# Feed-forward blocks of a four-layer hybrid network: gate and up products made token-first or feature-first

## The chip, the cores and the metric

The kernel runs on one core of one Trainium2 chip, as a single program without communication. The metric is the device time of one execution in microseconds; less is better. A core has a matrix engine (TensorE, PE in the profile, with its weight loads listed apart as PEld), a vector engine (VectorE, DVE), a scalar engine (ScalarE, ACT), GpSimd (POOL), and a queue that issues DMA transfers (SyncE, SP).

## The reference, cut to what matters

```python
D_MODEL = 1024; SEQ = 256; DEPTH = 4; D_FF = 2816; FFN_HALF = 0.5

def swiglu(x, w_gate, w_up, w_down):
    return (jax.nn.silu(x @ w_gate) * (x @ w_up)) @ w_down

def reference(x, norm_pre, norm_post, ffn_w_gate, ffn_w_up, ffn_w_down, ...):
    for i in range(DEPTH):
        f = swiglu(rms_norm(x, norm_pre[i, 0]), ffn_w_gate[i, 0], ffn_w_up[i, 0], ffn_w_down[i, 0])
        x = x + FFN_HALF * rms_norm(f, norm_post[i, 0])
        hn = rms_norm(x, norm_pre[i, 1])
        ...  # one of three attention mixers m, by i % 3
        x = x + rms_norm(m, norm_post[i, 1])
        f = swiglu(rms_norm(x, norm_pre[i, 2]), ffn_w_gate[i, 1], ffn_w_up[i, 1], ffn_w_down[i, 1])
        x = x + FFN_HALF * rms_norm(f, norm_post[i, 2])
    return x
```

There are 256 tokens, a model width of 1024 and 2816 inner features. Each layer has two feed-forward blocks, so the program has eight, with an attention mixer between the two blocks of a layer (dilated, differential, sliding-window, and dilated again).

## The kernel before, in words

**Precision.** Every float32 operand of a matmul is split into a high and a low part of type fp32r, and `mm3` (lines 173 to 176) makes one product from three matmuls: high by high (L174), high by low (L175), low by high (L176). The first operand of `mm3` is the stationary one and its second is the moving one. In the profile's names the moving operand stands first: `gu<-hi,xT` has weights moving and xT stationary, `qk<-xT,hi` has xT moving and weights stationary.

**Weights.** They come in units of 128 x 2048 values (1 MB) in an order fixed in advance. `load_next` puts a DMA on the SP queue into one of three `raw` buffers; `split_next` makes `hi` on ACT (L141) and `lo` on DVE, or on POOL for some units (L142), in two pieces (four on POOL), into four rotating buffers each. `done(i)` is called after the last matmul of a unit: it splits the unit four ahead into the buffers that come free, and loads the next.

**A feed-forward block.** `norm_tr` transposes the normed input to `xT` (high and low, 8 row groups of 128 model features by 256 tokens each). `new_xT` starts it 48 elements into its buffer in the mixers and at 0 in the feed-forward blocks. `ffn` then works through the inner features in six chunks c, five of 512 and a last one of 256. Within a chunk it makes the gate product for the two halves of the tokens, t = 0 and 1 (PSUM banks of tag mm, three of them), then the up product (banks of tag s, two). xT is stationary, 128 tokens at a time, and 512 columns of weights move: 8 row groups x 3 matmuls for each of two halves and two products, 96 matmuls per chunk. `gate` applies silu on ACT (L360), `up` multiplies on DVE (L365) to `h`, with tokens on the partitions. `transposes` turns `h` back on TensorE (four transposes of 128 columns for each half, two in the last chunk, L373), and ACT and DVE write the result as `hTh` and `hTl` (L376, L377). The transposes of chunk c - 1 are issued in chunk c between the first and the second weight unit of its gate product; those of the last chunk come after the first unit of `closing`.

**closing** multiplies hT (stationary) by the 11 units of the down weights (512 columns moving, `acc`), adds to the residual `x` and prepares the next stage's norm. It is the same for feed-forward blocks and mixers.

**Mixers.** They issue their input projections in pieces between attention work. Query and key projections (`qk`) have the weights stationary and 256 columns of xT moving; value projections (`v`) of the dilated mixer have xT stationary and 384 columns of weights moving. Score products (`sc`), transposes (`tp`) and value products (`o`) stand between these pieces. Each engine has its instructions in one order, fixed when the program is built.

Of the kernel before, what the change touches and what calls it, by code (L numbers as in the profile page):

```python
# [8 lines left out]
F32 = mybir.dt.float32  # L9
F32R = mybir.dt.float32r  # L10
BF16 = mybir.dt.bfloat16
AF = mybir.ActivationFunctionType
ALU = mybir.AluOpType

P = 128
SEQ = 256
D = 1024
DFF = 2816
KD = D // P
# [26 lines left out]
def tile_network(  # L46
# [27 lines left out]
    act, dve, pe, pool = nc.scalar, nc.vector, nc.tensor, nc.gpsimd  # L74
# [7 lines left out]
    def bank(tag, name):  # L82
        return ps.tile([P, 512], F32, tag=tag, name=name, bufs={"mm": 3, "s": 2, "tr": 2, "o": 1}[tag])
# [61 lines left out]
    def take(n=1):  # L145
        i = state["use"]
        state["use"] += n
        return list(range(i, i + n))
# [3 lines left out]
    def pump(n=99):  # L152
        while pending and n:
            n -= 1
            i = pending.pop(0)
            split_next()
            load_next()
            for f in hooks.pop(i, []):
                f()

    def done(i, later=False):
        his.pop(i)
        los.pop(i)
        pending.append(i)
        if not later:
            pump()

    def wview(i, k):
        w = units[i].shape[-1]
        return (his[i][:, :w].rearrange("p (k n) -> p k n", k=k),  # L170
                los[i][:, :w].rearrange("p (k n) -> p k n", k=k))

    def mm3(o, a, b, first, last):
        pe.matmul(o, lhsT=a[0], rhs=b[0], start=first, stop=False)  # L174
        pe.matmul(o, lhsT=a[0], rhs=b[1], start=False, stop=False)  # L175
        pe.matmul(o, lhsT=a[1], rhs=b[0], start=False, stop=last)  # L176
# [18 lines left out]
    xT = {}  # L195

    NX, NH = KD * SEQ, KF * SEQ

    def two(z, o, n):

        return [z[:, o + i * n:o + (i + 1) * n].rearrange("p (k n) -> p k n", n=SEQ) for i in range(2)]

    def new_xT(s):
        z = actp.tile([P, 2 * NX + 64], F32R, tag="xT", name="xT")
        xT["h"], xT["l"] = two(z, 48 if s % 3 == 1 else 0, NX)

    def xt(k, t):
        sl = slice(t * P, (t + 1) * P) if t is not None else slice(0, SEQ)
# [15 lines left out]
    hn_of = {}  # L224

    def norm_elem(t, s, parts=1):

        ss = small.tile([P, 1], F32, tag="ssx", name="ssx")
        hn = actp.tile([P, D], F32, tag="w", name="hn", bufs=3)
        act.activation(out=hn, in_=x[:, t], func=AF.Square, scale=1.0 / 32.0, accum_out=ss)  # L230
        r = rstd_of(ss, None)
        state["norm"] = state["rstd"]
        for c in range(parts):
            cs = slice(c * D // parts, (c + 1) * D // parts)
            i = dve.scalar_tensor_tensor(out=hn[:, cs], in0=x[:, t, cs], scalar=r, in1=gains["pre", s][:, cs],
                                     op0=ALU.mult, op1=ALU.mult)
        hn_of[t] = hn, s
        return i

    def boundary_elem(t, s, acc, mid):  # L240
# [30 lines left out]
            return norm_tr_(t)  # L271

    def norm_tr_(t):
        hn, s = hn_of.pop(t)
        if t == 0:
            new_xT(s)
        for g in range(2):
            tp = bank("tr", "tp")
            for j in range(4):
                k = 4 * g + j  # L280
                pe.transpose(tp[:, j * P:(j + 1) * P], hn[:, k * P:(k + 1) * P], ident)
            tv = tp.rearrange("p (i n) -> p i n", i=4)
            h = xT["h"][:, 4 * g:4 * g + 4, t * P:(t + 1) * P]
            i = act.copy(out=h, in_=tv)
            dve.tensor_tensor(out=xT["l"][:, 4 * g:4 * g + 4, t * P:(t + 1) * P], in0=tv,
                              in1=h.bitcast(F32), op=ALU.subtract)
        return i
# [56 lines left out]
    def ffn(layer, which):  # L344
        s = 3 * layer + 2 * which
        with ExitStack() as c:
            fp = c.enter_context(tc.tile_pool(name="ffn", bufs=2, reuse_waits="tile"))
            hTh, hTl = two(fp.tile([P, 2 * NH], F32R, name="hT", bufs=1), 0, NH)
            hs = {}

            def mm_unit(i, k, k0, o, t, mid=None):
                wh, wl = wview(i, k)
                for kk in range(k):
                    if mid and kk == k // 2:
                        mid()
                    mm3(o, xt(k0 + kk, t), (wh[:, kk], wl[:, kk]), k0 + kk == 0, k0 + kk == KD - 1)

            def gate(c, t, g, w):
                sg = fp.tile([P, 512], F32, tag="sg", name="sg")
                act.activation(out=sg[:, :w], in_=g[:, :w], func=AF.Silu)  # L360
                return sg

            def up(c, t, sg, u, w):
                h = fp.tile([P, 512], F32, tag="h", name="h")
                dve.tensor_tensor(out=h[:, :w], in0=sg[:, :w], in1=u[:, :w], op=ALU.mult)  # L365
                hs[c, t] = h

            def transposes(c, t):
                h = hs.pop((c, t))
                n = 4 if c < 5 else 2  # L370
                tp = bank("tr", "tp")
                for i in range(n):
                    pe.transpose(tp[:, i * P:(i + 1) * P], h[:, i * P:(i + 1) * P], ident)  # L373
                tv = tp[:, :n * P].rearrange("p (i n) -> p i n", i=n)
                d = hTh[:, 4 * c:4 * c + n, t * P:(t + 1) * P]
                act.copy(out=d, in_=tv)  # L376
                dve.tensor_tensor(out=hTl[:, 4 * c:4 * c + n, t * P:(t + 1) * P], in0=tv,  # L377
                                  in1=d.bitcast(F32), op=ALU.subtract)


            ids = take(4)
            for t in range(2):
                g, u = bank("mm", "g"), bank("s", "u")
                for m in range(2):
                    mm_unit(ids[m], 4, 4 * m, g, t)
                    if t:
                        done(ids[m])
                sg = gate(0, t, g, 512)
                for m in range(2):
                    mm_unit(ids[2 + m], 4, 4 * m, u, t, (lambda: norm_tr(1)) if t == 0 and m == 1 else None)  # L390
                    if t:
                        done(ids[2 + m])
                up(0, t, sg, u, 512)
            for c in range(1, 6):
                w = 512 if c < 5 else 256
                k = 4 if c < 5 else 8
                sgs = []
                for part in range(2):
                    o = [bank("mm" if part == 0 else "s", "gu") for _ in range(2)]
                    ids = take(KD // k)  # L400
                    for m, i in enumerate(ids):
                        for t in range(2):
                            mm_unit(i, k, k * m, o[t][:, :w], t)
                        done(i)
                        if part == 0 and m == 0:
                            transposes(c - 1, 0)
                            transposes(c - 1, 1)
                    for t in range(2):
                        if part == 0:
                            sgs.append(gate(c, t, o[t], w))  # L410
                        else:
                            up(c, t, sgs[t], o[t], w)

            def between(m):
                if m == 0:
                    transposes(5, 0)
                    transposes(5, 1)

            for _ in closing(s, lambda k, t: (hTh[:, k, t * P:(t + 1) * P], hTl[:, k, t * P:(t + 1) * P]),
                             11, 4, between, lambda m, t: True):  # L420
                pass


# [583 lines left out]
    if True:  # L1007
# [10 lines left out]
        with tc.high_priority(PRI):  # L1018
            i = norm_elem(0, 0, 2)
            j = norm_tr(0)  # L1020
# [69 lines left out]
def _rows(w, k):  # L1090

    import numpy as np

    lead = w.shape[:-2]
    n = w.shape[-1]
    w = w.reshape(*lead, k, P, n)
    w = np.moveaxis(w, -3, -2)
    return w.reshape(*lead, P, k * n)


def _pack(inp):
# [9 lines left out]
    ffn = np.empty((8, 33, P, 2048), A["ffn_w_gate"].dtype)  # L1111
    wg = A["ffn_w_gate"].reshape(8, D, DFF)
    wu = A["ffn_w_up"].reshape(8, D, DFF)
    wd = A["ffn_w_down"].reshape(8, DFF, D)
    for c in range(5):
        cs = slice(512 * c, 512 * c + 512)
        for p, w in enumerate((wg, wu)):
            for m in range(2):
                ffn[:, 4 * c + 2 * p + m] = _rows(w[:, 512 * m:512 * m + 512, cs], 4)
    ffn[:, 20] = _rows(wg[:, :, 2560:], 8)  # L1120
    ffn[:, 21] = _rows(wu[:, :, 2560:], 8)
    ffn[:, 22:] = _rows(wd.reshape(8, 11, 256, D), 2)
    r["w_ffn"] = ffn

# [59 lines left out]
```

## Time and profile before

| | |
|---|---|
| median of 3 runs | 2312.66 us (2312.63 to 2313.06) |
| profiled execution | 2313.26 us, span 2311.4 us |
| mean granted TensorE clock | 0.998 of 2.4 GHz |
| PE busy in the span | 2278.0 us (99%) |
| PEld, DVE, ACT, POOL busy | 87%, 54%, 52%, 27% |
| read from HBM | 401.5 MB, 174 GB/s over the span |

A matmul's listed duration includes its way through the array, and consecutive matmuls overlap, so the listed durations add up to more than the time that passes. What a matmul costs in a stream is the distance from its start to the next one's start; this text calls it the pitch. The profiled execution has 1.9 us outside its span.

### The profile page before, as it was taken

The page shows a single profiled execution, that of the slowest core. Times are in us where ns is not written, and L with a number is a line of the kernel's source. Part 1 is how long each engine was busy: PE and PEld are TensorE (multiplying, and loading weights), DVE is VectorE, ACT ScalarE, POOL GpSimd, SP SyncE. Part 2 cuts the span into 40 slices and gives each one's busy share as a digit, 9 for nine tenths or more (in the row PEclk, how much of TensorE's full clock was granted, in tenths as well). Part 3 has the DMA queues.
Part 4 walks back from the last instruction along what each step waited for, and adds up shares of the span by engine and source line. Part 5 has one row for each costly group of instructions (what it writes and reads, how often), then busy time and mean ns, then how long its engine had stood idle before and what let it go on. Part 6 is the DMA issues. An engine that isn't in the chain of part 4 may idle for free.

```text
span 2311.4 us, 32467 instructions
## 1 busy us (share of the span) xinstructions
PE 2278.0 (99%) x12912; PEld 1999.4 (87%) x12912; DVE 1252.8 (54%) x1830; ACT 1199.0 (52%) x2102; POOL 634.0 (27%) x640
## 2 busy tenths in 40 slices
PE   8999999999999999999999999999999999999998
PEld 6888999988888889788888887788888899998887
DVE  6545544565455555565465558655655544446553
ACT  5435666654444446654354448544444466666442
POOL 0004877620020028620020024100200287773000
PEclk9999999999999999999999999999999999999999
DMA  7554444445545544255555542555555544343552
GB/s 286 185 186 172 171 151 151 155 182 182 182 183 211 183 162 176 92 218 182 185 203 188 187 169 92 191 191 182 190 192 183 190 169 151 140 156 139 216 182 91
DMA packets 60498, 404.65 MB, mean 175 GB/s; under 512 B 6965, under 2 KB 7866, under 8 KB 16314
## 3 DMA queue, kind: packets, MB, share of 16 engines
q1 hardware_dynamic: 60202, 402.51, 47.9%
q8 instruction: 101, 1.65, 0.3%
q14 instruction: 51, 0.42, 0.1%
q10 hardware_dynamic: 144, 0.07, 0.0%
HBM read 401.50 MB, written 1.05 MB: 174 GB/s over the span
## 4 chain that ended last, share of the span: by engine, by line
PE 91%; DVE 3%; POOL 2%; ACT 2%; issue 1%; DMA 1%; SPq 0%; POOLq 0%; DVEq 0%; ACTq 0%
PE gu L175 11%; PE gu L176 11%; PE gu L174 11%; PE acc L176 8%; PE acc L174 8%; PE acc L175 7%; PE qk L175 4%; PE qk L174 4%; PE qk L176 4%; PE v L174 2%; PE v L175 2%; PE v L176 2%; PE tp L373 2%; PE tp L816 2%; POOL lo L142 1%; DVE lo L142 1%
## 5 line engine op out<-in xcount | busy, mean ns | idle before, releaser
L141 ACT CAST hi<-raw 128x1024 fp32r<-128x1024 f32 (+2 forms) x970 | 776.1, 845 | 765.5 <-PE gu L176 322.5
L142 DVE TENSOR_TENSOR lo<-raw,hi 128x1024 fp32r<-128x1024 f32 (+1 forms) x546 | 661.5, 1250 | 549.6 <-ACT hi L141 549.3
L142 POOL TENSOR_TENSOR lo<-raw,hi 128x512 fp32r<-128x512 f32 (+1 forms) x424 | 546.7, 1324 | 147.7 <-ACT hi L141 147.4
L174 PE MATMUL gu<-hi,xT 128*128 128x512 f32 (+1 forms) x1280 | 474.2, 370 | 0.0
L176 PE MATMUL gu<-hi,xT 128*128 128x512 f32 (+1 forms) x1280 | 471.0, 368 | 0.0
L175 PE MATMUL gu<-lo,xT 128*128 128x512 f32 (+1 forms) x1280 | 471.0, 368 | 0.0
L219 POOL TENSOR_SCALAR ms<-ssf 128x1 f32<-128x1 f32 x24 | 7.2, 302 | 1418.9 <-ACT junk L249 1417.9
L176 PE MATMUL acc<-hi,hT 128*128 128x512 f32 x704 | 276.1, 392 | 0.0
L175 PE MATMUL acc<-lo,hT 128*128 128x512 f32 x704 | 275.9, 392 | 0.0
L176 PEld LDWEIGHTS gu<-hi,xT 128*128 128x128 f32 x1280 | 241.3, 188 | 40.0
L174 PE MATMUL acc<-hi,hT 128*128 128x512 f32 x704 | 275.6, 391 | 0.0
L174 PEld LDWEIGHTS gu<-hi,xT 128*128 128x128 f32 x1280 | 241.4, 189 | 39.2
L175 PEld LDWEIGHTS gu<-lo,xT 128*128 128x128 f32 x1280 | 241.4, 189 | 39.1
L174 PE MATMUL qk<-xT,hi 128*128 128x256 f32 x800 | 225.7, 282 | 0.0
L175 PE MATMUL qk<-xT,hi 128*128 128x256 f32 x800 | 222.8, 279 | 0.0
L176 PE MATMUL qk<-xT,lo 128*128 128x256 f32 x800 | 222.7, 278 | 0.0
L176 PEld LDWEIGHTS acc<-hi,hT 128*128 128x128 f32 x704 | 132.2, 188 | 28.4
L175 PEld LDWEIGHTS acc<-lo,hT 128*128 128x128 f32 x704 | 132.2, 188 | 27.8
L174 PEld LDWEIGHTS acc<-hi,hT 128*128 128x128 f32 x704 | 132.3, 188 | 26.2
L174 PEld LDWEIGHTS qk<-xT,hi 128*128 128x128 f32 x800 | 151.3, 189 | 0.2
L176 PEld LDWEIGHTS qk<-xT,lo 128*128 128x128 f32 x800 | 150.6, 188 | 0.1
L175 PEld LDWEIGHTS qk<-xT,hi 128*128 128x128 f32 x800 | 150.3, 188 | 0.2
(265 smaller groups left out, 3364.6 us busy)
## 6 DMA issues: line engine op xcount, KB each, us to landing
raw<-in_w_ffn_dram SPq DMA_DIRECT2D x263, 1024.0 KB, 4.8
raw<-in_w_a_qk_dram SPq DMA_DIRECT2D x48, 1024.0 KB, 4.8
raw<-in_w_a_v_dram SPq DMA_DIRECT2D x32, 768.0 KB, 4.2
raw<-in_w_a_out_dram SPq DMA_DIRECT2D x8, 1024.0 KB, 4.8
raw<-in_w_b_qk_dram SPq DMA_DIRECT2D x8, 1024.0 KB, 4.8
gain<-in_g_pre_dram SPq DMA_DIRECT2D x12, 512.0 KB, 6.1
gain<-in_g_post_dram SPq DMA_DIRECT2D x12, 512.0 KB, 7.2
raw<-in_w_b_v_dram SPq DMA_DIRECT2D x4, 1024.0 KB, 4.8
```

Source lines behind the costliest of these rows:

```text
L141: act.copy(out=hi[:, cs], in_=r[:, cs])
L142: eng.tensor_tensor(out=lo[:, cs], in0=r[:, cs], in1=hi[:, cs].bitcast(F32), op=ALU.subtract)
L174: pe.matmul(o, lhsT=a[0], rhs=b[0], start=first, stop=False)
L175: pe.matmul(o, lhsT=a[0], rhs=b[1], start=False, stop=False)
L176: pe.matmul(o, lhsT=a[1], rhs=b[0], start=False, stop=last)
L219: pool.tensor_scalar(out=ms, in0=a, scalar1=b, scalar2=EPS, op0=ALU.add, op1=ALU.add)
L373: pe.transpose(tp[:, i * P:(i + 1) * P], h[:, i * P:(i + 1) * P], ident)
L816: pe.transpose(tp[:, c0:c0 + P], src, ident)
```

## The change

Only the first 512 inner features are still made with xT stationary and transposed. The other 2304 are made in nine chunks of 256 features, c = 2 to 10, with the weights stationary and all 256 tokens of xT moving. The two halves f of 128 features lie side by side in one PSUM bank, features on the partitions, so the product comes out in the layout that `closing` wants; ACT copies `h` from SBUF to `hTh` and DVE makes `hTl` from `h` and `hTh`, without a transpose. Weights are packed to match, a unit being 256 features by all 1024 model features. xT always starts 48 elements into its buffer.

```diff
-    def new_xT(s):
+    def new_xT():
         z = actp.tile([P, 2 * NX + 64], F32R, tag="xT", name="xT")
-        xT["h"], xT["l"] = two(z, 48 if s % 3 == 1 else 0, NX)
+        xT["h"], xT["l"] = two(z, 48, NX)
...
-            for c in range(1, 6):
-                w = 512 if c < 5 else 256
-                k = 4 if c < 5 else 8
-                sgs = []
+            for c in range(2, 11):
                 for part in range(2):
-                    o = [bank("mm" if part == 0 else "s", "gu") for _ in range(2)]
-                    ids = take(KD // k)
-                    for m, i in enumerate(ids):
-                        for t in range(2):
-                            mm_unit(i, k, k * m, o[t][:, :w], t)
-                        done(i)
-                        if part == 0 and m == 0:
-                            transposes(c - 1, 0)
-                            transposes(c - 1, 1)
-                    for t in range(2):
-                        if part == 0:
-                            sgs.append(gate(c, t, o[t], w))
-                        else:
-                            up(c, t, sgs[t], o[t], w)
-
-            def between(m):
-                if m == 0:
-                    transposes(5, 0)
-                    transposes(5, 1)
+                    i, = take()
+                    wh, wl = wview(i, KD)
+                    o = bank("s" if part else "mm", "gu")
+                    for f in range(2):
+                        fs = slice(f * P, (f + 1) * P)
+                        for k in range(KD):
+                            mm3(o[:, f * SEQ:(f + 1) * SEQ], (wh[:, k, fs], wl[:, k, fs]), xt(k, None),
+                                k == 0, k == KD - 1)
+                    done(i)
+                    if part == 0:
+                        sg = gate(o)
+                        if c == 2:
+                            transposes(0)
+                            transposes(1)
+                h = up(sg, o)
+                hv = h.rearrange("p (f n) -> p f n", f=2)
+                d = hTh[:, 2 * c:2 * c + 2]
+                act.copy(out=d, in_=hv)
+                dve.tensor_tensor(out=hTl[:, 2 * c:2 * c + 2], in0=hv, in1=d.bitcast(F32), op=ALU.subtract)
 
             for _ in closing(s, lambda k, t: (hTh[:, k, t * P:(t + 1) * P], hTl[:, k, t * P:(t + 1) * P]),
-                             11, 4, between, lambda m, t: True):
+                             11, 4, lambda m: None, lambda m, t: True):
                 pass
...
-    for c in range(5):
-        cs = slice(512 * c, 512 * c + 512)
-        for p, w in enumerate((wg, wu)):
-            for m in range(2):
-                ffn[:, 4 * c + 2 * p + m] = _rows(w[:, 512 * m:512 * m + 512, cs], 4)
-    ffn[:, 20] = _rows(wg[:, :, 2560:], 8)
-    ffn[:, 21] = _rows(wu[:, :, 2560:], 8)
+    for p, w in enumerate((wg, wu)):
+        for m in range(2):
+            ffn[:, 2 * p + m] = _rows(w[:, 512 * m:512 * m + 512, :512], 4)
+        for c in range(2, 11):
+            ffn[:, 2 * c + p] = _rows(w[:, :, 256 * c:256 * c + 256], 8)
```

## Rows read from the trace of the kernel before

**Rows 1.** The page: busy time, share and count of each engine.
```profile
PE 2278.0 (99%) x12912; PEld 1999.4 (87%) x12912; DVE 1252.8 (54%) x1830; ACT 1199.0 (52%) x2102; POOL 634.0 (27%) x640
```
**Rows 2.** The page: the chain of waits, shares by engine.
```profile
PE 91%; DVE 3%; POOL 2%; ACT 2%; issue 1%; DMA 1%; SPq 0%; POOLq 0%; DVEq 0%; ACTq 0%
```
**Rows 3.** Busy time by stretch: chunks 1 to 5 of the third block.
```profile
core 0: us, PE busy (x) PEld busy (x) DVE busy (x) ACT busy (x) POOL busy (x), PEclk, DMA share, GB/s
505.74:608.73 102.99, 102.99 (x521) 87.75 (x520) 55.49 (x57) 45.95 (x56) 0.00 (x0) 1.00 0.54 199
```
**Rows 4.** PE's timeline, chunk 1 of that block: start, duration, operation.
```profile
510.95 0.39 PE L176 MATMUL gu<-hi,xT 128*128 128x512 f32 x1
511.19 1.03 PE L373 MATMUL tp<-ident,h 128*128 128x128 f32 x8
511.98 0.48 PE L174 MATMUL gu<-hi,xT 128*128 128x512 f32 x1
512.29 0.40 PE L175 MATMUL gu<-lo,xT 128*128 128x512 f32 x1
...
533.61 0.39 PE L176 MATMUL gu<-hi,xT 128*128 128x512 f32 x1
```
**Rows 5.** PE's timeline, chunk 5, 256 columns of weights moving.
```profile
596.35 0.28 PE L174 MATMUL gu<-hi,xT 128*128 128x256 f32 x1
...
601.99 0.28 PE L176 MATMUL gu<-hi,xT 128*128 128x256 f32 x1
...
603.10 0.28 PE L175 MATMUL gu<-lo,xT 128*128 128x256 f32 x1
...
608.61 0.28 PE L176 MATMUL gu<-hi,xT 128*128 128x256 f32 x1
```
**Rows 6.** PE's timeline, dilated mixer: transposes, then 256 columns of xT moving.
```profile
302.36 0.60 PE L816 MATMUL tp<-ident,sp 128*128 128x128 f32 x4
302.71 0.37 PE L174 MATMUL qk<-xT,hi 128*128 128x256 f32 x1
...
303.04 0.28 PE L176 MATMUL qk<-xT,lo 128*128 128x256 f32 x1
...
308.14 0.28 PE L176 MATMUL qk<-xT,lo 128*128 128x256 f32 x1
```
**Rows 7.** The same stage, a stretch that follows score products.
```profile
230.97 0.28 PE L174 MATMUL qk<-xT,hi 128*128 128x256 f32 x1
...
237.92 0.28 PE L176 MATMUL qk<-xT,lo 128*128 128x256 f32 x1
```
**Rows 8.** The same stage, 384 columns of weights moving, later straight into qk.
```profile
250.07 0.34 PE L176 MATMUL v<-hi,xT 128*128 128x384 f32 x1
...
252.15 0.34 PE L176 MATMUL v<-hi,xT 128*128 128x384 f32 x1
...
257.64 0.28 PE L175 MATMUL qk<-xT,hi 128*128 128x256 f32 x1
...
258.81 0.28 PE L176 MATMUL qk<-xT,lo 128*128 128x256 f32 x1
```
**Rows 9.** The same stage, one of the stretches after transposes.
```profile
262.36 0.60 PE L816 MATMUL tp<-ident,sp 128*128 128x128 f32 x4
...
262.92 0.28 PE L175 MATMUL qk<-xT,hi 128*128 128x256 f32 x1
...
266.45 0.28 PE L175 MATMUL qk<-xT,hi 128*128 128x256 f32 x1
```
**Rows 10.** PE's timeline, closing of the third block: the last chunk's transposes.
```profile
613.97 0.39 PE L176 MATMUL acc<-hi,hT 128*128 128x512 f32 x1
614.20 0.60 PE L373 MATMUL tp<-ident,h 128*128 128x128 f32 x4
...
614.87 0.39 PE L175 MATMUL acc<-lo,hT 128*128 128x512 f32 x1
```
**Rows 11.** Groups by line and shape: ACT copies, busy us, mean ns, idle before.
```profile
L141 ACT CAST hi<-raw 128x512 fp32r<-128x512 f32 x312 | 180.4, 620 | 39.6 <-issue 21.9 <-PE qk L175 8.9 <-DMA raw<-in_w_ffn_dram 3.5
...
L376 ACT CAST hT<-tp 128x512 fp32r<-128x512 f32 x80 | 42.5, 581 | 0.0
```

More of the change, by code (lines that the diff above doesn't have):

```diff
@@ L236, in norm_elem @@
                                      op0=ALU.mult, op1=ALU.mult)
-        hn_of[t] = hn, s
+        hn_of[t] = hn
         return i
@@ L273, in norm_tr_ @@
     def norm_tr_(t):
-        hn, s = hn_of.pop(t)
+        hn = hn_of.pop(t)
         if t == 0:
-            new_xT(s)
+            new_xT()
         for g in range(2):
@@ L356, in mm_unit, with gate, up, transposes @@
                     mm3(o, xt(k0 + kk, t), (wh[:, kk], wl[:, kk]), k0 + kk == 0, k0 + kk == KD - 1)
-            def gate(c, t, g, w):
+            def gate(g):
                 sg = fp.tile([P, 512], F32, tag="sg", name="sg")
-                act.activation(out=sg[:, :w], in_=g[:, :w], func=AF.Silu)
+                act.activation(out=sg, in_=g, func=AF.Silu)
                 return sg
-            def up(c, t, sg, u, w):
+            def up(sg, u):
                 h = fp.tile([P, 512], F32, tag="h", name="h")
[L365 to L370, printed above, removed]
+                dve.tensor_tensor(out=h, in0=sg, in1=u, op=ALU.mult)
+                return h
+            def transposes(t):
+                h = hs.pop(t)
                 tp = bank("tr", "tp")
-                for i in range(n):
+                for i in range(4):
                     pe.transpose(tp[:, i * P:(i + 1) * P], h[:, i * P:(i + 1) * P], ident)
-                tv = tp[:, :n * P].rearrange("p (i n) -> p i n", i=n)
-                d = hTh[:, 4 * c:4 * c + n, t * P:(t + 1) * P]
+                tv = tp.rearrange("p (i n) -> p i n", i=4)
+                d = hTh[:, :4, t * P:(t + 1) * P]
                 act.copy(out=d, in_=tv)
-                dve.tensor_tensor(out=hTl[:, 4 * c:4 * c + n, t * P:(t + 1) * P], in0=tv,
-                                  in1=d.bitcast(F32), op=ALU.subtract)
+                dve.tensor_tensor(out=hTl[:, :4, t * P:(t + 1) * P], in0=tv, in1=d.bitcast(F32),
+                                  op=ALU.subtract)
             ids = take(4)
@@ L387, in ffn @@
                         done(ids[m])
-                sg = gate(0, t, g, 512)
+                sg = gate(g)
                 for m in range(2):
@@ L392, in ffn @@
                         done(ids[2 + m])
-                up(0, t, sg, u, 512)
-            for c in range(1, 6):
-                w = 512 if c < 5 else 256
-                k = 4 if c < 5 else 8
-                sgs = []
-                for part in range(2):
-                    o = [bank("mm" if part == 0 else "s", "gu") for _ in range(2)]
-                    ids = take(KD // k)
-                    for m, i in enumerate(ids):
-                        for t in range(2):
-                            mm_unit(i, k, k * m, o[t][:, :w], t)
-                        done(i)
-                        if part == 0 and m == 0:
-                            transposes(c - 1, 0)
-                            transposes(c - 1, 1)
-                    for t in range(2):
-                        if part == 0:
-                            sgs.append(gate(c, t, o[t], w))
-                        else:
-                            up(c, t, sgs[t], o[t], w)
@@ L414, in between @@
-            def between(m):
-                if m == 0:
-                    transposes(5, 0)
-                    transposes(5, 1)
+                hs[t] = up(sg, u)
+            for c in range(2, 11):
+                for part in range(2):
+                    i, = take()
[17 more added lines that the diff above has]
+                dve.tensor_tensor(out=hTl[:, 2 * c:2 * c + 2], in0=hv, in1=d.bitcast(F32), op=ALU.subtract)
```

## The prediction

> **What bounds the kernel.** I read the page first: PE is busy 99% of the span, the next engine 54% [rows 1], and the chain that ended last lies on PE for 91% of its length [rows 2]. So the time is what PE's queue takes, and the view to read next is that queue in the stage of the change. In chunks 1 to 5 of the third block PE is busy for the whole 102.99 us, at a granted clock of 1.00 (2.4 GHz), while DVE has work for 54% of it, ACT for 45% and POOL for none [rows 3]. A block's change in time is then the change in what its matmuls and transposes occupy on PE, as long as the other engines keep their slack. The third view is PE's timeline, read for pitches, because listed durations overlap: a 512-column matmul is listed with 0.39 us but the next starts after 21.32 us / 94 = 226.8 ns [rows 4]. Apart from the odd matmul after an interruption, that is 226.7 ns.
>
> **What is removed.** In chunks 1 to 5 of each block: 4 x 96 = 384 matmuls of 512 columns, 96 of 256 columns, and five groups of eight transposes.
> - 384 x 226.7 ns = 87.05 us.
> - The 256-column matmuls of the last chunk: 5.64 us / 47 = 120.0 ns before its transposes and 5.51 us / 46 = 119.8 ns after them [rows 5]; all 16 such stretches have this pitch. 96 x 120.0 = 11.52 us.
> - A group of eight transposes: from the matmul before it to the second one after it 1.34 us pass, where two pitches would be 0.45 [rows 4]: 0.89 us, five times, 4.45 us.
>
> The sum, 103.0 us, agrees with the stage's 102.99 [rows 3]. One group (chunk 0's) stays, four go. In closing the last group, of four, goes as well: 0.90 us less two pitches, 0.45 us [rows 10].
>
> **What is added.** Nine chunks x 2 products x 2 halves of features x 8 x 3 = 864 matmuls of 256 columns, weights stationary and xT moving at offset 48. The same columns stream in total (864 x 256 = 384 x 512 + 96 x 256), so everything hangs on the pitch. This form does exist in the trace: it is `qk` in the mixers, with the same buffers and the same offset. It shows two pitches, and each holds over a whole stretch:
> - 113.3 ns (5.10 us / 45) after transposes [rows 6], over the change of half and of weight unit. This is half of 226.7.
> - 117.8 ns (6.95 us / 59) after score products [rows 7]: all 42 stretches of the dilated mixers that follow five score matmuls have it, up to 60 matmuls long.
>
> Of the 37 stretches that follow transposes 32 settle at 113.3 and five stay at 117.8; rows 9 are one of these, 3.53 us / 30. Straight after a stream with the roles exchanged, without transposes between, it is 117 ns, 1.17 us / 10 [rows 8]. So the pitch isn't that of the shape alone; it depends on how the stream was entered, and then stays. In the changed block the stream is entered from 512-column matmuls with roles exchanged, and after 48 matmuls it is interrupted by chunk 0's eight transposes; from there 816 matmuls run with no score product or transpose among them. I take 117.8 for the first 48 (nearest rows 8; bounds 113.3 and 120.0) and 113.3 for the 816, the case of rows 6. Bounds for these are 113.3 and 120.0.
>
> 48 x 117.8 ns + 816 x 113.33 ns + 0.88 us for the group that stays = 5.65 + 92.48 + 0.88 = 99.0 us; against 102.99 that saves 3.98 us, and with closing 4.43.
>
> A rule speaks against cutting the columns. The Trainium skill, TensorE: Matmul & The Clock Gate, section Back-to-back issue gap, gives 262 cycles for 256 columns and 518 for 512: two halves cost 6 cycles, or 2.5 ns, more than the whole, since each matmul carries a fixed part. By the rule, 384 pairs x 8 blocks would take back 7.7 us of the gain. Rows 4 and 6 show no such part: the starts are given to 0.01 us, so 45 pitches leave room for 0.2 ns each, and 384 pairs x 0.4 ns x 8 = 1.2 us.
>
> **What moves.** Chunk 0 keeps its 96 matmuls of 512 columns with xT stationary, but xT now starts at offset 48. No row has 512 columns so. The nearest, 384 columns with xT stationary at offset 48, has 2.08 us / 12 = 173.3 ns [rows 8], where 226.7 x 384 / 512 would be 170.0. I take that excess of 3.3 ns: 96 x 3.3 = 0.32 us lost; bounds nothing and twice that in proportion, the 6.7 ns by which 120.0 exceeds 113.3, 0.64 us.
>
> **Costed at nothing.** ACT and DVE have per 512 features the same two silus, two products, two copies and two subtractions. The copy's source becomes SBUF, for which the nearest row is 620 ns against 581 from PSUM [rows 11]: nine copies x 39 ns = 0.35 us per block, on an engine that is idle for 57 us of the stage [rows 3]. If that cover were gone, the first to be late would be the split of the unit four ahead, which PE needs only three units (16.3 us) later; the copy that waits for `up` stands in ACT's queue ahead of the next unit's split, and it waits for two subtractions of `lo` and the product, three DVE instructions of on average 55.49 / 57 = 0.97 us [rows 3], which is over within the 5.4 us that a unit lasts. Banks: a chunk takes one of tag mm and one of s where it took two of each, so each bank has longer to come free. The last hT pieces are needed at closing's eleventh unit, the earlier ones long before. Weight units keep their number, size and order on SP's queue, at 199 GB/s here [rows 3].
>
> **Sum.** Per block 3.98 + 0.45 - 0.32 = 4.11 us, times 8 = 32.9. From the profiled execution's 2313.26 us: 2280.4. That execution is 0.6 us above the median of the runs, so I say 2280. This case's own bounds (first 48 at 113.3 or 120.0, chunk 0 at nothing or 0.64) are 2276 to 2284.
>
> **Rivals.**
> 1. *The stream stays at 117.8 ns* [rows 7, 9] in every block, because nothing after the first transposes shakes it out. 864 x 117.8 + 0.88 = 102.66; saved 0.33 + 0.45 - 0.32 = 0.46 us per block, 3.7 in all: 2309.6. For it: five of the 37, and a gap before the long stream that is much like theirs. Against: 32 of 37.
> 2. *Slower: the weight load takes over.* A weight load of 128 columns must follow each 256-column matmul; transposes, 128 columns moving with a load each, start 108 ns apart (eight last 0.43 us longer than four [rows 4, 10]) where 128 columns alone would be 226.7 / 4 = 57, so about 108 ns is the load's own pace, and 113.3 leaves it little. If load and stream hinder each other as in rows 5, the pitch is 120.0 and stays there: 864 x 120.0 + 0.88 = 104.56 us, per block 1.57 more - 0.45 + 0.32 = 1.44, in all 11.5 us: 2324.8. It decides from a pitch of (102.99 - 0.88 + 0.13) / 864 = 118.3 ns on, only 0.5 above rival 1. For it: all 16 stretches of rows 5, transposes or not. Against: they have the roles exchanged and xT at offset 0; no qk stretch has 120. The Trainium skill, same page, section LDWEIGHTS, puts a load of 128 columns at 107 ns; the trace's 108 agrees.
> 3. *A part of the gain*: some blocks settle at 113.3 and others at 117.8; four of each give 2280.4 + 4 x (4.11 - 0.46) = 2295. For it: the qk stretches after transposes don't all settle alike. Against: the 16 stretches of rows 5 do, and the eight blocks issue the same instructions. A fixed part of each matmul would also lower the gain; the rows leave it 1.2 us, inside the forecast's range. By the Trainium skill's figure above the time would be 2288.
> 4. *The change doesn't act*, since another engine's lateness replaces PE's work: 2313. Against: the slack above.
>
> **Chances.** Forecast 0.68; part of the gain 0.11; rival 1 0.10; rival 2 0.10; rival 4 0.01. What a measurement here can tell from no change is 0.2%, 4.6 us, so below 2308.0 is faster: forecast and rival 3, 0.79. Rivals 1 and 4 are within it: 0.11. Slower: 0.10. The range runs from the forecast's lower bound, with 2 us for what isn't seen, to rival 1: 2274 to 2310; the forecast's own, 2276 to 2284.
>
> **What would show it.** The pitch of `gu<-xT,hi` after the transposes in each block: 113.3 for the forecast, 117.8 rival 1, 120 rival 2, two values among blocks rival 3. The stretch from chunk 0's last matmul to the first `acc` should be 99.0 us instead of 103.0. `g` and `u` of chunk 0 should have 230 ns. No row of `tp<-ident,h` should stand beyond eight per block, and PE should have no wait for ACT or DVE there. I would be wrong above all if the pitch in a run of 816 isn't what a run of 48 shows.

## The result, and the profile after

| | before | after |
|---|---|---|
| median | 2312.64 us, 4 runs (2312.24 to 2313.06) | 2284.53 us, 4 runs (2280.66 to 2287.67) |
| profiled execution | 2313.26 us | 2287.67 us, span 2285.8 us |

The ratio of the times is 0.9876 (95% interval 0.9863 to 0.9888): 28.1 us faster, where 32.9 were forecast, and well clear of the 0.2% that a measurement here can tell. One thing is new in the runs themselves. Those of before lie within 0.8 us, those of after stand at 2280.7, twice 2284.5, and 2287.7, in steps of 3 to 4 us. In the later comparisons, on two other occasions, the runs of before spread over 3.1 and 2.8 us, so steps of this size are only a hint.

The page of after, busy time of each engine and then the shares of the chain of waits, answers to [rows 1, 2]:

```profile
PE 2253.5 (99%) x15696; PEld 2097.1 (92%) x15696; DVE 1253.8 (55%) x1814; ACT 1195.0 (52%) x2086; POOL 633.7 (28%) x640
...
PE 91%; DVE 4%; ACT 2%; POOL 2%; DMA 1%; issue 1%; SPq 0%; POOLq 0%; DVEq 0%; ACTq 0%
```

PE has 2784 instructions more and 24.5 us less to do; it is still the bound, and DVE and ACT have what they had. The change acts on PE alone, as intended. Busy time by stretch, answering to [rows 3], for the first four of the eight blocks (from the first `gu` matmul to the first `acc`), and last the closing of the second of them. The block that [rows 3 to 5] and [rows 10] call the third is this second feed-forward block, the third stage of the program:

```profile
core 0: us, PE busy (x) PEld busy (x) DVE busy (x) ACT busy (x) POOL busy (x), PEclk, DMA share, GB/s
36.13:134.97 98.84, 98.84 (x873) 98.83 (x872) 56.44 (x63) 48.47 (x58) 0.00 (x0) 1.00 0.57 205
500.70:603.14 102.44, 102.44 (x873) 102.43 (x872) 55.43 (x56) 45.54 (x55) 0.00 (x0) 1.00 0.54 197
687.77:786.61 98.84, 98.84 (x874) 98.84 (x873) 55.42 (x56) 45.60 (x55) 0.00 (x0) 1.00 0.56 204
1003.66:1106.10 102.44, 102.44 (x873) 102.44 (x872) 55.34 (x56) 45.54 (x55) 0.00 (x0) 1.00 0.54 196
603.14:663.98 60.84, 60.84 (x274) 50.22 (x273) 29.75 (x26) 26.29 (x35) 6.91 (x7) 1.00 0.43 157
```

The same instructions take 98.84 us in one block and 102.44 in the next. Of the eight, the second, fourth and seventh take 102.44, the others 98.84. In every one PE is busy for the whole stretch and the granted clock is 1.00, so neither a wait nor the clock makes the difference. It stands in the pitch. PE's timeline (start, duration, operation) of the second block, which is slow; this answers to [rows 4]:

```profile
495.20 0.39 PE L174 MATMUL u<-hi,xT 128*128 128x512 f32 x1
...
500.47 0.40 PE L176 MATMUL u<-hi,xT 128*128 128x512 f32 x1
500.70 0.28 PE L174 MATMUL gu<-xT,hi 128*128 128x256 f32 x1
...
506.05 0.28 PE L176 MATMUL gu<-xT,lo 128*128 128x256 f32 x1
506.16 1.03 PE L372 MATMUL tp<-ident,h 128*128 128x128 f32 x8
506.95 0.36 PE L174 MATMUL gu<-xT,hi 128*128 128x256 f32 x1
507.15 0.28 PE L175 MATMUL gu<-xT,hi 128*128 128x256 f32 x1
...
603.02 0.28 PE L176 MATMUL gu<-xT,lo 128*128 128x256 f32 x1
```

And of the first block, which is fast:

```profile
41.49 0.28 PE L176 MATMUL gu<-xT,lo 128*128 128x256 f32 x1
41.60 1.04 PE L372 MATMUL tp<-ident,h 128*128 128x128 f32 x8
42.39 0.37 PE L174 MATMUL gu<-xT,hi 128*128 128x256 f32 x1
42.59 0.28 PE L175 MATMUL gu<-xT,hi 128*128 128x256 f32 x1
...
134.86 0.28 PE L176 MATMUL gu<-xT,lo 128*128 128x256 f32 x1
```

After the transposes 814 pitches take 95.87 us in the slow block, 117.8 ns each, and 92.27 us in the fast one, 113.4 each. These are the two pitches of `qk` [rows 6, 7], each held from the first few matmuls to the last. The difference, 816 x 4.4 ns, is the 3.6 us between the blocks and about the step between the runs. The first 48 matmuls take 5.35 us / 47 = 113.8 ns here, entry included; they settle at 113.3 in all eight blocks. Chunk 0, now at offset 48, has 5.27 us / 23 = 229.1 ns.

The sum then closes. A fast block gains 4.15 us in its stretch (102.99 - 98.84), a slow one 0.55; closing gains 0.49 (61.33 us before, 60.84 after); chunk 0's stretch loses 0.15 (22.95 before, 23.10 after). 5 x 4.49 + 3 x 0.89 = 25.1 us, of 25.6 between the two profiled executions.

### The profile page after: what moved, and what is told of

Its sections match the earlier page's. It is cut to its first block, busy times and chain, and to the rows that moved or that the text cites. A ratio compares the mean times of both kernels' runs of the same rounds, so it can differ in the third digit from the quotient of the medians.

```text
span 2285.8 us, 38031 instructions
## 1 busy us (share of the span) xinstructions
PE 2253.5 (99%) x15696; PEld 2097.1 (92%) x15696; DVE 1253.8 (55%) x1814; ACT 1195.0 (52%) x2086; POOL 633.7 (28%) x640
## 4 chain that ended last, share of the span: by engine, by line
PE 91%; DVE 4%; ACT 2%; POOL 2%; DMA 1%; issue 1%; SPq 0%; POOLq 0%; DVEq 0%; ACTq 0%
PE gu L175 12%; PE gu L174 12%; PE gu L176 12%; PE acc L176 8%; PE acc L174 8%; PE acc L175 8%; PE qk L174 4%; PE qk L175 4%; PE qk L176 4%; PE v L174 2%; PE v L175 2%; PE v L176 2%; PE tp L813 2%; DVE lo L142 1%; PE u L176 1%; PE u L175 1%
## 5 line engine op out<-in xcount | busy, mean ns | idle before, releaser
L174 PE MATMUL gu<-xT,hi 128*128 128x256 f32 x2304 | 640.8, 278 | 0.0
L175 PE MATMUL gu<-xT,hi 128*128 128x256 f32 x2304 | 640.1, 278 | 0.0
L176 PE MATMUL gu<-xT,lo 128*128 128x256 f32 x2304 | 640.0, 278 | 0.0
L174 PEld LDWEIGHTS gu<-xT,hi 128*128 128x128 f32 x2304 | 436.0, 189 | 0.3
L175 PEld LDWEIGHTS gu<-xT,hi 128*128 128x128 f32 x2304 | 432.6, 188 | 0.4
L176 PEld LDWEIGHTS gu<-xT,lo 128*128 128x128 f32 x2304 | 432.5, 188 | 0.0
L176 PE MATMUL acc<-hi,hT 128*128 128x512 f32 x704 | 276.0, 392 | 0.0
L175 PE MATMUL acc<-lo,hT 128*128 128x512 f32 x704 | 275.9, 392 | 0.0
L174 PE MATMUL acc<-hi,hT 128*128 128x512 f32 x704 | 274.6, 390 | 0.0
L174 PE MATMUL qk<-xT,hi 128*128 128x256 f32 x800 | 226.1, 283 | 0.0
L176 PE MATMUL qk<-xT,lo 128*128 128x256 f32 x800 | 223.2, 279 | 0.0
L175 PE MATMUL qk<-xT,hi 128*128 128x256 f32 x800 | 223.2, 279 | 0.0
L175 PEld LDWEIGHTS acc<-lo,hT 128*128 128x128 f32 x704 | 132.2, 188 | 28.1
L176 PEld LDWEIGHTS acc<-hi,hT 128*128 128x128 f32 x704 | 132.2, 188 | 28.1
L174 PEld LDWEIGHTS acc<-hi,hT 128*128 128x128 f32 x704 | 132.3, 188 | 26.4
L174 PEld LDWEIGHTS qk<-xT,hi 128*128 128x128 f32 x800 | 151.6, 190 | 0.2
L176 PEld LDWEIGHTS qk<-xT,lo 128*128 128x128 f32 x800 | 151.0, 189 | 0.1
L175 PEld LDWEIGHTS qk<-xT,hi 128*128 128x128 f32 x800 | 150.8, 189 | 0.2
```

## The experiments

The first four kernels below ran on one chip (the kernel before: 2313.10 us, 14 runs, 2311.86 to 2314.91), the other four on another (2313.43 us, 7 runs, 2312.34 to 2315.17). What they had to tell apart: what decides a block's pitch, and what the offset of xT has to do with it.

### Chunk 0's transposes near the stream's end

```diff
-                        if c == 2:
-                            transposes(0)
-                            transposes(1)
+                    elif c == 9:
+                        transposes(0)
+                        transposes(1)
```

`h` of chunk 0 gets buffers of its own, so that it can wait. Now 768 matmuls run before the transposes and 96 after them.

> Chunk 0's transposes are issued late, after the up product of chunk 9, so that the long stream of 256-column matmuls is entered straight from chunk 0's 512-column matmuls and runs 768 matmuls undisturbed. Theory A (the pitch is settled in the first few matmuls after a stream is entered and then held; the entry after transposes can go either way, the entry without them went to 113.3 ns in all eight blocks of the profile): all eight blocks at 113.3 ns up to the transposes; 3 x 3.6 us less than the profiled execution of the changed kernel, 2277 us, with at most 0.4 us per block for the last 96 matmuls, and the same time in every run to within 2 us. Theory B (the pitch belongs to the block: in the profile the three blocks at 117.8 are exactly those whose first weight unit has an odd number, so which of the rotating weight buffers the stream starts in decides): the same three blocks stay at 117.8, 2284 to 2288 us.

Measured: 2279.59 us (4 runs, 2277.91 to 2281.07), ratio 0.9852 (0.9837 to 0.9867). All eight streams of 768 have 113.3 ns. The 96 after the transposes have 117.8 in two blocks and 113.3 in six. PE's timeline of one of the two:

```profile
684.72 0.40 PE L176 MATMUL u<-hi,xT 128*128 128x512 f32 x1
684.96 0.28 PE L174 MATMUL gu<-xT,hi 128*128 128x256 f32 x1
...
772.02 1.03 PE L372 MATMUL tp<-ident,h 128*128 128x128 f32 x8
772.81 0.36 PE L174 MATMUL gu<-xT,hi 128*128 128x256 f32 x1
773.01 0.28 PE L175 MATMUL gu<-xT,hi 128*128 128x256 f32 x1
...
784.08 0.28 PE L176 MATMUL gu<-xT,lo 128*128 128x256 f32 x1
```

87.06 us / 768 = 113.4 ns up to the transposes, 11.07 us / 94 = 117.8 after them, in one block and with the same xT: it is the interruption that may leave the stream slow. Theory A holds and B falls. The profiled execution, 2279.87, is 2.9 us above the expected 2277: two slow ends cost 2 x 96 x 4.4 ns = 0.8, and the rest lies outside the blocks (the first chunk took 25.57 us against 24.65 in after's profile, the third mixer's first part 56.58 against 55.08). The runs spread over 3.2 us, where theory A had expected 2; the slow ends, 0.4 us each, and the parts outside the streams both move the time.

### The same transposes one weight unit later

```diff
-                        if c == 2:
-                            transposes(0)
-                            transposes(1)
+                    elif c == 2:
+                        transposes(0)
+                        transposes(1)
```

> Chunk 0's transposes are issued one weight unit later than in the changed kernel (after chunk 2's up product instead of its gate product), so the long stream is entered in the next of the four rotating weight buffers. Theory B (the buffer decides): the three blocks that were at 117.8 ns are now at 113.3 and the five others can be at 117.8, up to 5 x 3.4 us above 2277: up to 2294 us. Theory A (the draw falls on entry, whatever the buffer): the first 96 matmuls at 113.3 in all blocks, after the transposes each block at 113.3 or 117.8 with no tie to the unit's number; time in steps of 3.4 us above 2277, about 2277 to 2288.

Measured: 2284.25 us (4 runs, 2284.04 to 2287.34), ratio 0.9875 (0.9861 to 0.9890): as the change itself. In the profile the slow blocks are now the fifth and the seventh. Busy time by stretch, a fast block (the second, slow in after) and a slow one (the fifth, fast in after):

```profile
501.30:600.10 98.80, 98.80 (x873) 98.80 (x872) 55.24 (x56) 45.59 (x55) 0.00 (x0) 1.00 0.57 203
1183.90:1286.10 102.20, 102.20 (x873) 102.20 (x872) 55.33 (x56) 45.53 (x55) 0.00 (x0) 1.00 0.54 196
```

The slow block is 3.40 us longer, 768 x 4.43 ns, since 96 matmuls now come before the transposes. In after's profile all slow blocks began with an odd weight unit, which had suggested the position in the rotating buffers (B); here one of the two begins with an even one. Which buffer the weights lie in doesn't decide.

### The change without its moved offset

```diff
-        xT["h"], xT["l"] = two(z, 48, NX)
+        xT["h"], xT["l"] = two(z, 48 if s % 3 == 1 else 0, NX)
```

> The changed kernel with xT at offset 0 in the feed-forward blocks and 48 in the mixers, as before. Theory A with collisions of two reads (the stationary and the moving operand hinder each other for some distances between their addresses, which is why the last chunk of the kernel before had 120 ns): all 864 matmuls per block at 120 ns whatever the entry, chunk 0 back at 226.7 ns: per block 104.6 + 0 instead of 102.99 + 0.45, together 2322 us. If the offset does nothing for the 256-column stream: two pitches as in the changed kernel, and chunk 0 back at 226.7: 2275 to 2286 us.

Measured: 2321.36 us (5 runs, 2320.53 to 2322.61), ratio 1.0034 (1.0020 to 1.0047): slower than before. All 864 matmuls of all eight blocks are at 120.0 ns, before and after the transposes, and chunk 0 is back at 226.7. PE's timeline, from the second matmul after the transposes to the last of the stream:

```profile
513.77 0.28 PE L175 MATMUL gu<-xT,hi 128*128 128x256 f32 x1
...
611.45 0.28 PE L176 MATMUL gu<-xT,lo 128*128 128x256 f32 x1
```

97.68 us / 814 = 120.0 ns, the pitch of [rows 5] with the roles exchanged. So the change without its offset loses 8 us here; the offset, which the diff moves in one line, turns that into a gain of 28.

### The kernel before with the moved offset

```diff
-        xT["h"], xT["l"] = two(z, 48 if s % 3 == 1 else 0, NX)
+        xT["h"], xT["l"] = two(z, 48, NX)
```

> The kernel before with xT at offset 48 everywhere: the moved part alone. If what chunk 0 showed after the change (229.0 ns for 512 columns at offset 48) holds for all chunks: 480 x 2.3 ns = 1.1 us per block more, the last chunk at 117.8 instead of 120 0.2 us less, together 2320 us. If the last chunk settles at 113.3: 2317. If transposes let the 512-column stream settle at 226.7 again: 2308 to 2313.

Measured: 2318.05 us (10 runs, 2317.03 to 2320.70), ratio 1.0021 (1.0011 to 1.0030). The 512-column chunks are at 229.0, also after transposes; the last chunk, with 256 columns of weights moving, has 113.3 in six blocks and 117.8 in two before its transposes, and 117.8 in all after them, so the time lies between the 2317 and the 2320 that were expected for the one and the other. PE's timeline, chunk 1 of the second block:

```profile
513.37 0.40 PE L175 MATMUL gu<-lo,xT 128*128 128x512 f32 x1
...
534.90 0.39 PE L176 MATMUL gu<-hi,xT 128*128 128x512 f32 x1
```

21.53 us / 94 = 229.0 ns: 2.3 more than at offset 0 [rows 4]. The same offset that speeds up 256 columns slows down 512, so neither half of the change gains by itself: the shape alone costs 8 us, the offset alone 5, both together gain 28.

### The transposes in closing

```diff
-                        if c == 2:
-                            transposes(0)
-                            transposes(1)
...
+            def between(m):
+                if m == 0:
+                    transposes(0)
+                    transposes(1)
```

Chunk 0's features are numbered last in hT, the down weights are packed in that order, and `closing` transposes them after its first weight unit, where the kernel before had the last chunk's. The stream of 864 is not interrupted. The same 512 features are still transposed.

> Chunk 0's features are numbered last (the down weights' rows are packed in that order), so its eight transposes can stand in the closing stage after its first unit, where 512-column matmuls follow; the long stream of 864 is never interrupted. Theory A (a stream's pitch is settled at its entry and held; entered from 512-column matmuls it went to 113.3 ns in all 24 cases so far): all eight blocks at 113.3 ns to the end, 98.0 us for the stream, no step of 3.4 us between runs: 2277 us, and about 0.4 us per slow end less than with the transposes after chunk 9. Rival (C: the pitch can also change inside a long stream, or the entry from 512 columns is a draw too, only with better odds): in some runs a block at 117.8, 3.8 us each: 2277 to 2285.

Measured: 2276.84 us (4 runs, 2276.38 to 2277.70), ratio 0.9842 (0.9827 to 0.9856): the fastest version, 7.7 us below the change, and its runs lie within 1.3 us, without steps. All eight blocks are at 113.3. Busy time by stretch, a block that was slow in after with its closing, and one more block:

```profile
500.46:598.41 97.95, 97.95 (x865) 97.94 (x864) 54.21 (x54) 44.61 (x53) 0.00 (x0) 1.00 0.57 205
598.41:660.14 61.73, 61.73 (x283) 51.03 (x281) 30.97 (x28) 27.29 (x37) 6.94 (x7) 1.00 0.44 156
1183.28:1281.23 97.95, 97.95 (x866) 97.95 (x865) 54.22 (x54) 44.62 (x53) 0.00 (x0) 1.00 0.58 205
```

97.95 + 61.73 = 159.68 us, and a fast block of after has 98.84 + 60.84 = 159.68. The transposes cost the same 0.89 us in either place; what is gained is that no block is slow. The profile alone doesn't prove it, since its blocks 2 to 8 all lack the mark of a block that would have been slow (told under the next experiment). Two blocks with that mark ran 768 matmuls at 113.3 in the first experiment, and there the slow pitch came only after the transposes.

### Three matmuls of 512 columns after the transposes

```diff
                             transposes(1)
+                            z = bank("o", "kick")
+                            mm3(z, xt(0, 1), [v[i][:, :512] for v in (his, los)], True, True)
```

They have xT stationary and weights moving; nobody reads their result. `gate` and `done` of that unit stand behind them in the program.

> The changed kernel with three matmuls of 512 columns (xT stationary, weights moving, into a bank that nobody reads) put behind chunk 0's transposes, so the long stream is entered from the same kind of matmul as the first 48. Theory A1 (what stands directly before the stream decides): all eight blocks at 113.3 ns; 8 x 0.7 us for the added matmuls on top of 2277: 2283 us in every run. Theory A2 (the transposes put the stream out of step and only time in the stream before them decides): two or three blocks remain at 117.8: 2290 to 2294 us.

Measured: 2281.43 us (4 runs, 2280.85 to 2282.20), ratio 0.9860 (0.9844 to 0.9877). All eight long streams are at 113.3, also the two that in the trace's finer digits left their first 48 with an interval of 118 ns ahead of the transposes. That interval, 117 or 118 ns, had marked the later slow blocks in after and in the two experiments that move the transposes (24 streams, no exception; 115 ns ahead of those that then ran at 113.3). In these two blocks A1 holds and A2 falls.

The mark goes back further. In the same finer digits the starts of chunk 0's last 48 matmuls, of 512 columns, follow each other in a pattern of three, in one of two orders: about 226, 229 and 232 ns after a matmul of L174, L175 and L176, or 232, 226 and 229. In blocks 2 to 8 of those three traces all seven streams at 117.8 come after the second order and all fourteen at 113.3 after the first. The two marked blocks here have the second order too. The first block, whose chunk 0 is issued in other pieces, had the second order in the two experiments and ran at 113.3 all the same. So which blocks will be slow is mostly settled before the stream of 256 columns begins, and the transposes bring it out.

PE's timeline of one of the two marked blocks:

```profile
1191.78 1.03 PE L372 MATMUL tp<-ident,h 128*128 128x128 f32 x8
1192.57 0.48 PE L174 MATMUL kick<-hi,xT 128*128 128x512 f32 x1
1192.89 0.40 PE L175 MATMUL kick<-lo,xT 128*128 128x512 f32 x1
1193.12 0.39 PE L176 MATMUL kick<-hi,xT 128*128 128x512 f32 x1
1193.36 0.28 PE L174 MATMUL gu<-xT,hi 128*128 128x256 f32 x1
1193.47 0.28 PE L175 MATMUL gu<-xT,hi 128*128 128x256 f32 x1
...
1285.73 0.28 PE L176 MATMUL gu<-xT,lo 128*128 128x256 f32 x1
```

Busy time of the same stretch, its columns as above:

```profile
1186.32:1285.84 99.52, 99.52 (x876) 99.38 (x875) 56.20 (x56) 45.67 (x55) 0.00 (x0) 1.00 0.55 201
```

92.26 us / 814 = 113.3 ns. The three extra matmuls cost 0.68 us per block (99.52 - 98.84) and save 3.60 in each block that would have been slow. With the weights stationary at offset 48, entry from 512 columns gave 113.3 in all 48 cases (eight each of after and of three of these kernels, sixteen here). With the roles exchanged it doesn't always: the last chunk of the kernel before with the moved offset comes straight from 512 columns too, and has 117.8 in two blocks of eight.

### Two other offsets

```diff
-        xT["h"], xT["l"] = two(z, 48, NX)
+        xT["h"], xT["l"] = two(z, 16, NX)
```

> xT at offset 16 elements (64 bytes) everywhere instead of 48. Theory of two reads that hinder each other by the distance of their addresses: another pitch or another share of blocks at each offset; at 16 anything from 113.3 in all blocks (about 2277) to 120 in all (2322). The mixers' products read the same xT and move too. If only the step from 0 to not 0 counts: as at 48, two to three blocks at 117.8, 2281 to 2288.

```diff
-        xT["h"], xT["l"] = two(z, 48, NX)
+        xT["h"], xT["l"] = two(z, 32, NX)
```

> xT at offset 32 elements (128 bytes) everywhere. As at 16: by the distance of addresses 2277 to 2322 with one pitch or two; if only the step from 0 to not 0 counts, as at 48, 2281 to 2288.

Measured, one run each: 2313.09 us at offset 16 and 2327.18 us at 32. Both lie outside 2281 to 2288, so more than the step from 0 to not 0 counts, and 32 lies above the 2322 that was expected at worst. Busy time by stretch, one block at offset 16:

```profile
506.22:608.86 102.64, 102.64 (x873) 102.63 (x872) 55.36 (x56) 45.58 (x55) 0.00 (x0) 1.00 0.55 196
```

And two blocks at offset 32:

```profile
510.67:614.06 103.39, 103.39 (x874) 103.39 (x872) 55.37 (x56) 45.54 (x55) 0.00 (x0) 1.00 0.55 195
698.90:803.45 104.55, 104.55 (x874) 104.55 (x872) 55.38 (x56) 45.56 (x55) 0.00 (x0) 1.00 0.53 193
```

(102.64 - 0.88) / 864 = 117.8 ns at 16, 118.7 or 120.0 at 32. With the other runs, in the feed-forward blocks:

| offset of xT | 256 columns, weights stationary | 512 columns, xT stationary |
|---|---|---|
| 0 | 120.0 ns | 226.7 ns |
| 16 | 117.8 | 233.3 |
| 32 | 118.7 or 120.0 | 232.2 to 233.4 |
| 48 | 113.3 or 117.8 | 229.0 |

The mixers share the offset and slow down as well (the first takes 252.27 us at 32, 248.04 at 48). Where xT starts in its row changes the pitches, but it doesn't settle them alone. In the same trace at offset 16, where all eight blocks have 117.8, twelve `qk` stretches of 48 matmuls after transposes in the dilated mixers have 113.3. PE's timeline of one, from its second matmul to its last:

```profile
294.08 0.28 PE L175 MATMUL qk<-xT,hi 128*128 128x256 f32 x1
...
299.29 0.28 PE L176 MATMUL qk<-xT,lo 128*128 128x256 f32 x1
```

5.21 us / 46 = 113.3 ns. So 113.3 occurs at 16 as well as at 48; at 32 no stretch of either kind has it, and at 0 only the feed-forward blocks were run. Whether the place of xT counts by itself or its distance from the weights is not shown, since no run moves the weights.

## Why the prediction was right, and what it mis-sized

- **PE is the bound, and the other engines' work is hidden**: right. PE has no wait in a block's stretch, which is 100% PE in all eight; ACT (45.5 us) and DVE (55.4) have there what they had [rows 3].
- **What is removed**: right. The removed parts were read to 0.01 us of the stage, and closing gave back 0.49 us where 0.45 was forecast.
- **The pitch of the new stream**: the mechanism was right. It has exactly two pitches, 113.3 and 117.8, taken up at its entry after the transposes and then held over 816 matmuls as over 48. The step that failed is the size taken for the 816: 113.33 ns in all eight blocks. Three of the profiled execution's eight had 117.8, 3 x 3.6 = 10.8 us. With those at 113.3 it would have been 2276.9; the version that transposes in closing has all eight there and is profiled at 2277.7.
- **The case that came is rival 3**, a part of the gain, with five and three blocks in place of four and four. It was given 0.11 because "the eight blocks issue the same instructions". That argument fell: they do, and settle differently, from block to block and, by the steps in the runs' times, from run to run. The rows had said so. Five of 37 `qk` stretches stayed slow after transposes; read as a chance per block they give (32/37)^8 = 0.31 for no slow block among eight. That reading is rough: four of the five stand at the same two places of the two dilated mixers, and these four are slow in every trace here in which the mixers' xT is at 48, so the stretches are no independent draws.
- **The first 48 matmuls**: taken at 117.8 after [rows 8], they run at 113.3 in every block. That is 48 x 4.5 ns = 0.2 us per block, 1.7 in all, on the good side. The 1.17 us of those rows came after 384-column matmuls, not 512.
- **Chunk 0 at offset 48**: 0.32 us was taken, 0.15 lost by its stretch and 96 x 2.4 ns = 0.23 by its pitch; 0.7 to 1.4 us in all, also on the good side. These two make up for part of the slow blocks, which may be why the median missed by no more than 4.5 us; that they cancel is luck.
- **Rival 2, 120.0 ns**: it was close. It names what happens at offset 0, in every block, and its 2324.8 us compares with 2321.36 measured. The remark that the 120.0 in [rows 5] came with offset 0 was the one that counted, and the roles, given beside it, did not: with roles exchanged and offset 48 the last chunk also has 113.3 or 117.8.
- **A fixed part of each matmul**: not seen. 814 pitches of 113.3 ns against 226.7 / 2 leave less than 0.1 ns. The prediction worked out 2.5 ns per pair from the Trainium skill, TensorE: Matmul & The Clock Gate, section Back-to-back issue gap, which gives its cycles for an isolated matmul.

Shown: the pitch is taken up where the stream is entered and kept; transposes ahead may leave it slow and 512-column matmuls did not, with the weights stationary; the weight buffer doesn't decide; the offset changes the pitches, though not alone. Only argued: that the count of slow blocks makes the steps among the runs that have no profile (their 2280.7, 2284.5 and 2287.7 fit one, two and three). Open: what gives chunk 0's matmuls the one order or the other, and with it picks a block's state; and why the offset acts. That the reads of the two operands hinder each other stays a conjecture, since no run here measures them apart.

## What to carry to other kernels

When a change swaps which operand stands still, the start address of the operands is a part of the change: try a few offsets, since here the same instructions take 2284.5 us at offset 48 and 2327.2 at 32. Read a pitch over every stretch, not as a mean, and where the trace shows two, price each block by the share of stretches at either; then look for a place for the interruption, such as a stage with long matmuls, where the stream isn't restarted by it. Runs that differ in equal steps can be a sign of such a state; only profiles show it.

## What was not expected of the hardware

- A stream of equal matmuls holds the pace at which it was entered: 113.3 or 117.8 ns, for 816 matmuls, at the same granted clock of 1.00 and without a wait. With three longer matmuls at its head all eight blocks ran at 113.3, the two that bore the mark of the 117.8 ns among them.
- The start of one operand in its row, moved by 16 to 48 elements, changes the pitch of 256-column matmuls between 113.3 and 120.0 ns and that of 512-column ones between 226.7 and 233.4, and what is best for the one (48) isn't for the other (0). The Trainium skill, TensorE: Matmul & The Clock Gate, section Back-to-back issue gap, has a table with one gap for each number of columns, for an isolated matmul; in the streams here one number of columns had several pitches, by the place of xT and by the entry.
